# A feed-forward up projection by seven half-size products: nine units instead of four, and their weight sums made by accumulating transfers

## The chip, the cores and the metric

The kernel runs on one core of one Trainium2 chip. The metric is the device time of one execution in microseconds (us), of which the median of three runs is taken. TensorE (PE) multiplies, VectorE (DVE) and ScalarE (ACT) do the elementwise work, GpSimd (POOL) and SyncE (SP) issue transfers: SP on a hardware queue, POOL on a queue whose descriptors software writes.

## The reference

One block of a hybrid model on 528 rows (16 meta tokens and 512 of the sequence), width 1024. All is f32:

```python
xn = rms_norm(h, norm_mix_g[l]); z = xn @ w_in[l]        # a gated linear recurrence and a
...                                                       # retention branch, mixed into h
h = h + mixed @ w_out[l]
xn = rms_norm(h, norm_ffn_g[l])
up = causal_dwconv(xn @ w_up[l], ffn_conv_w[l], ffn_conv_b[l])   # w_up: 1024 x 6144
gate, val = jnp.split(up, 2, axis=-1)
h = h + (jax.nn.gelu(gate) * val) @ w_down[l]             # w_down: 3072 x 1024
out = rms_norm(h, norm_final_g)[:, N_META:]
```

The change is in `xn @ w_up`, in its gate half.

## The kernel before, in words

Every f32 weight is used as two f16 parts, a high part and a remainder, and so is every activation; a product is three matmuls (high x high, high x rest, rest x high). `split` (lines 91 to 94) makes the two parts of a tile: ACT writes the high part (line 92), DVE then the rest (line 93). This is called a cut here.

Weights come in *units* of 1 MB or less, listed in the order of use. `unit_load` (line 187) loads the next unit on SP's queue (`load`, line 104) into a buffer of the pool `wraw` (`raw`, 128 x 2048 f32, two buffers) and queues its cuts, which write tiles of the pool `wsp` (`wt`, ten tiles). The cuts are not made at once: `tick` (line 310), called between the products, makes the next one as long as the tiles from the unit in use onwards are at most `ahead[0]` (6 in the up projection, 8 from j = 10 on). A plain unit takes two tiles and two cuts. The load of a unit is issued when the cuts of the unit before it begin (`u + 2`, line 294).

The up projection runs over j = 0 to 11. Each turn has two units of 8 x 128 rows by 256 columns: one of the gate half (two channels of 128 columns) and one of the value half. A plain turn (lines 1478 to 1490) makes four channels in the same way: `up_conv` runs 48 matmuls of 258 columns on both halves of the rows (line 418) and `conv` the convolution (once ACT, line 1375, twice DVE, line 1377); a gate channel then gets its gelu (line 1391), a value channel is multiplied with its gate (line 1487). `act_forms` (line 1323) cuts the results for the down projection.

In a *fast* turn (j in `FAST_UP`, line 28: 3, 5, 7, 9) the gate unit is computed as a 2 x 2 block product in seven half-size products instead of eight (`up_products`, line 1394): each is 12 matmuls of 258 columns (line 1399). The order on PE is B11, T3, T2, B21, T1, then the first value channel (`ps`), B22, T4, and the second value channel. Names are those of the weight block; B are blocks of the unit, T sums of blocks. Several of them accumulate in one PSUM bank `pa`: after B11 ACT copies it out (`kept`, line 1405), T2 is added on top and copied out (the second `kept`), T1 on top of that (`last`), then B22 (into `g`). DVE adds the pieces (line 1409).

The blocks and sums are made by `fast_steps` (line 237), in place in the raw buffer. top and low are its two halves of rows, left and right its two halves of columns:

```python
return [cut(top, left), cut(low, slice(0, 2 * bc)), sums,
        late(cut(top, slice(0, 2 * bc))), late(cut(low, slice(0, 2 * bc)))]
```

B11 is cut first, then the low half (B21, B22), then `sums` (lines 254 to 258) makes the four sums by three DVE additions (128 x 1024 and twice 128 x 512), and then the top half (T1, T3) and the low half (T4, T2) are cut. Four tiles, 3.5 of them cut. Gate and branch units ahead of the up projection and the units of the down projection are made the same way.

On each engine instructions run in the order in which they stand, and that order is fixed when the program is built. Semaphores make an instruction wait for another engine or for a transfer, and whatever stands behind it on its engine waits too. In the `order` fences below a number behind a name is that of the buffer's allocation, so raw_9953 is one unit's raw buffer and wt_10273 one cut tile.

Of the kernel before, what the change touches and what calls it, by code (L numbers as in the profile page):

```python
# [12 lines left out]
ALU = mybir.AluOpType  # L13
# [10 lines left out]
DFF = 3072  # L24
KF = DFF // P
T0 = NM - 2
TQ = T - T0
FAST_UP = (3, 5, 7, 9)
EPS = 1e-6

SW = 2.0 ** 8
# [20 lines left out]
def hybrid_block_kernel(ctx, tc, x, meta, norm_mix_g, w_in, conv_w, conv_b, rg_a_w, rg_a_b,  # L52
                        rg_x_w, rg_x_b, lam, w_brnn, w_bret, w_out, norm_ffn_g, w_up,
                        fconv_w, fconv_b, w_down, norm_final_g, rope_t, decay_t, out):
    nc = tc.nc
    const = ctx.enter_context(tc.tile_pool(name="const", bufs=1))
    xp = ctx.enter_context(tc.tile_pool(name="xp", bufs=4))
    pieces = ctx.enter_context(tc.tile_pool(name="pieces", bufs=46))
    wraw = ctx.enter_context(tc.tile_pool(name="wraw", bufs=2))
    wsp = ctx.enter_context(tc.tile_pool(name="wsp", bufs=10))  # L60
    work = ctx.enter_context(tc.tile_pool(name="work", bufs=8))
    small = ctx.enter_context(tc.tile_pool(name="small", bufs=4))
# [28 lines left out]
    def split(hi, lo, src, s):  # L91
        a = nc.scalar.activation(hi, src, AF.Copy, scale=s)  # L92
        b = nc.vector.scalar_tensor_tensor(lo, src, s, hi, op0=ALU.mult, op1=ALU.subtract)  # L93
        return a.ins, b.ins
# [3 lines left out]
    def load(dst, src):  # L98

        if last_load[0] is None:  # L100
            last_load[0] = nc.sync.dma_start(dst, src)
        else:
            with tc.issue_after(last_load[0].ins):
                last_load[0] = nc.sync.dma_start(dst, src)


    def kmaj(w, k0, nk, c0, ncol):
        return w[k0 * P:(k0 + nk) * P, c0:c0 + ncol].rearrange("(k p) c -> p k c", p=P)

    units = []  # L110

    def unit(nk, ncol, parts, fast=False):
        units.append((nk, ncol, parts, fast))
        return len(units) - 1

    o_ur, o_ug, o_q, o_k, o_v, o_gr, o_ga, o_gb = 0, 1280, 2560, 3584, 4608, 6656, 8704, 9728
# [1 line left out]
    for i in range(5):  # L118
        u = unit(8, 256, [(0, 0, kmaj(w_in, 0, 8, o_ur + 256 * i, 256))])
# [52 lines left out]
    u_out = [unit(2, 1024, [(0, 0, kmaj(w_out, 2 * a, 2, 0, 1024))]) for a in range(4)]  # L172
    u_up = []
    for j in range(12):
        u_up.append([unit(8, 256, [(0, 0, kmaj(w_up, 0, 8, a * DFF + 256 * j, 256))], fast=a == 0 and j in FAST_UP)
                     for a in range(2)])
    u_dn = []
    for ps_ in range(2):
        for q in range(6):
            rows = w_down[4 * q * P:(4 * q + 4) * P].rearrange("(i j p) c -> p j i c", i=2, j=2)  # L180
# [4 lines left out]
    loaded = []  # L185

    def unit_load(cuts=1):

        nk, ncol, parts, fast = units[len(loaded)]
        raw = wraw.tile([P, 2048], F32, name="raw")  # L190
        n = nk * ncol
        rv = raw[:, :n].rearrange("p (k c) -> p k c", k=nk)
        for k0, c0, ap in parts:
            load(rv[:, k0:k0 + ap.shape[1], c0:c0 + ap.shape[2]], ap)
        loaded.append(len(loaded))
        if fast:
            return fast_steps(rv, nk // 2, ncol // 2)
        hk = nk // 2
        hn = hk * ncol
        tiles = []  # L200

        def step(i, c):
            def run():
                if c == 0:
                    tiles.append(wsp.tile([P, 2, 1024], F16, name="wt"))
                sl = slice(c * hn // cuts, (c + 1) * hn // cuts)
                split(tiles[i][:, 0, sl], tiles[i][:, 1, sl], raw[:, i * hn:(i + 1) * hn][:, sl], SW)
            return run

        wviews.append(lambda a, k, c0, m: tiles[k // hk][:, a, k % hk * ncol + c0:k % hk * ncol + c0 + m])  # L210
        return [step(i, c) for i in range(2) for c in range(cuts)]

    def column_unit():

        _, ncol, parts, _ = units[len(loaded)]
        raw = wraw.tile([P, 2048], F32, name="raw")
        rv = raw.rearrange("p (k c) -> p k c", c=ncol)
        ap = parts[0][2]
        tiles = []

        def fetch(c):
            load(rv[:, :, c * P:c * P + P], ap[:, :, c * P:c * P + P])

        def step(i, c):
            def run():
                if c == 0:
                    tiles.append(wsp.tile([P, 2, 1024], F16, name="wt"))
                tv = [tiles[i][:, a].rearrange("p (k c) -> p k c", c=ncol)[:, :, c * P:c * P + P] for a in range(2)]
                split(tv[0], tv[1], rv[:, 4 * i:4 * i + 4, c * P:c * P + P], SW)
            return run  # L230

        loaded.append(len(loaded))
        wviews.append(lambda a, k, c0, m: tiles[k // 4][:, a, k % 4 * ncol + c0:k % 4 * ncol + c0 + m])
        queue([step(i, c) for c in range(2) for i in range(2)])
        return fetch

    def fast_steps(rv, bk, bc):


        tiles = []  # L240
        top, low = slice(0, bk), slice(bk, 2 * bk)
        left, right = slice(0, bc), slice(bc, 2 * bc)

        def cut(rows, cols):
            def run():
                t = wsp.tile([P, 2, 1024], F16, name="wt")
                src = rv[:, rows, cols]
                n = bk * src.shape[2]
                tv = [t[:, a, :n].rearrange("p (k c) -> p k c", k=bk) for a in range(2)]
                tiles.append(tv)  # L250
                split(tv[0], tv[1], src, SW)
            return run

        def sums():
            pair = rv[:, top].rearrange("p k (h c) -> p h k c", h=2)
            nc.vector.tensor_tensor(pair, pair, rv[:, :, right].rearrange("p (h k) c -> p h k c", h=2), op=ALU.add)  # L256
            nc.vector.tensor_tensor(rv[:, low, right], rv[:, top, left], rv[:, low, right], op=ALU.add)
            nc.vector.tensor_tensor(rv[:, low, left], rv[:, low, left], rv[:, low, right], op=ALU.add)  # L258

        at = {"B11": (0, 0), "B21": (1, 0), "B22": (1, bc), "T1": (2, 0), "T3": (2, bc), "T4": (3, 0), "T2": (3, bc)}  # L260

        def form(nm, a, k):
            i, c0 = at[nm]
            return tiles[i][a][:, k, c0:c0 + bc]

        def late(run):
            def behind():
                with behind_copy():
                    run()
            behind.late = True  # L270
            return behind

        wviews.append(form)
        return [cut(top, left), cut(low, slice(0, 2 * bc)), sums,
                late(cut(top, slice(0, 2 * bc))), late(cut(low, slice(0, 2 * bc)))]

# [4 lines left out]
    def behind_copy():  # L281

        return tc.issue_after(last_keep[0]) if gating[0] and last_keep[0] else nullcontext()

    done = [0]
    ahead = [6]
# [4 lines left out]

    def emit_step():
        u, run = steps[done[0]]
        while len(loaded) < min(u + 2, len(units)):
            queue(unit_load())
        run()
        done[0] += 1

    def queue(new):
        steps.extend((len(loaded) - 1, run) for run in new)  # L300
# [106 lines left out]
    def x_of(hi, lo):  # L407
        tv = (hi, lo)
        return lambda a, k, c0, n: tv[a][:, k, c0:c0 + n]
# [304 lines left out]
    for n in range(NR):  # L714
        ps = acc("ps")
        u, col = u_ug[n // 2], (n % 2) * P
# [587 lines left out]
            x2_whole(-1, None)  # L1304


    ahead[0] = 6
    x2f = x_of(x2h, x2l)
    HU = [(0, 258), (256, 258)]
    acts = []  # L1310
# [140 lines left out]
    def forms(n):  # L1451
        for _ in range(n if forming else 0):
            next(forming[0], None)

    for j in range(12):
        if j == 10:
            ahead[0] = 8
        wg, wu = get(u_up[j][0]), get(u_up[j][1])
        if j == 0:
            forming.append(x2_sums())  # L1460
        gates, vals = [], []
        if j in FAST_UP:
            run = up_products(wg)
            for n in range(5):
                next(run)
                if n in (3, 4):
                    flush(n - 2)
                tick()
            vals.append(up_conv(wu, 0, KF + 2 * j))
            tick()  # L1470
            g1 = gelu(conv(next(run), 2 * j + 1, True), -1.0)
            gates = [gelu(conv(next(run), 2 * j)), g1]
            vals.append(up_conv(wu, P, KF + 2 * j + 1))
            tick()
            for m in range(2):
                nc.vector.tensor_mul(vals[m][:, :SEQ], vals[m][:, :SEQ], gates[m][:, :SEQ])
        else:
            for m in range(2):
                gates.append(gelu(up_conv(wg, m * P, 2 * j + m)))
                (tick_behind_rows if j == 0 else tick)()  # L1480
                forms(1)
            for m in range(2):
                f = 2 * j + m
                if f == KF - 1:
                    psum_layout(bank=6, acc=1)
                cv = up_conv(wu, m * P, KF + f)
                nc.vector.tensor_mul(cv[:, :SEQ], cv[:, :SEQ], gates[m][:, :SEQ])
                vals.append(cv)
                (tick_behind_rows if j == 0 else tick)()
                forms(1)  # L1490
        pending.extend(act_forms(j, vals))
        if j + 1 not in FAST_UP:
            while pending:
                pending.pop(0)()
# [181 lines left out]
```

## Time and profile before

| | |
|---|---|
| Time, median of 3 runs | 1067.66 us (1067.13 to 1067.72) |
| Span of the profiled execution, first to last instruction | 1066.5 us |
| Median beside that span | 1.2 us more |
| DVE, ACT busy over the span | 853.2 us, 587.9 us |
| Mean granted TensorE clock | 0.998 |

The profile gives for each engine its busy time, for each stretch of time the same, the groups of equal instructions by line and shape, who waited for whom, and the chain of waits: the work that ended last, followed back. In a group's row the columns are line, engine, operation, output and input with shapes and count, then busy us and mean ns of one, then the idle time of the engine ahead of it and what ended it. In a row of the stretches the busy times of PE, PE's weight loads, DVE, ACT and POOL follow (with counts), then the granted clock, the share of the 16 DMA engines and GB/s. In a row of the transfers the last two numbers are KB and the median us from issue to landing.

### The profile page before, as it was taken

The page shows a single profiled execution, that of the slowest core. Times are in us where ns is not written, and L with a number is a line of the kernel's source. Part 1 is how long each engine was busy: PE and PEld are TensorE (multiplying, and loading weights), DVE is VectorE, ACT ScalarE, POOL GpSimd, SP SyncE. Part 2 cuts the span into 40 slices and gives each one's busy share as a digit, 9 for nine tenths or more (in the row PEclk, how much of TensorE's full clock was granted, in tenths as well). Part 3 has the DMA queues.
Part 4 walks back from the last instruction along what each step waited for, and adds up shares of the span by engine and source line. Part 5 has one row for each costly group of instructions (what it writes and reads, how often), then busy time and mean ns, then how long its engine had stood idle before and what let it go on. Part 6 is the DMA issues. An engine that isn't in the chain of part 4 may idle for free.

```text
span 1066.5 us, 20995 instructions
## 1 busy us (share of the span) xinstructions
PE 1048.0 (98%) x8995; PEld 851.1 (80%) x8995; DVE 853.2 (80%) x1301; ACT 587.9 (55%) x927; POOL 6.9 (1%) x20
## 2 busy tenths in 40 slices
PE   8999999999999999999999999999999999999997
PEld 6888888865685858887888885588888888888884
DVE  6884799998577878877797776479989897988965
ACT  8568954434364747655554454366566465454442
POOL 2000000000000000000000000000000000000000
PEclk9999999999999999999999999999999999999999
DMA  8341243431022312334433365032432324214322
GB/s 255 104 133 42 80 139 119 160 120 40 2 85 75 120 40 65 119 100 119 129 105 119 115 202 179 1 119 80 159 111 88 119 81 133 67 60 138 101 81 79
DMA packets 108989, 111.49 MB, mean 105 GB/s; under 512 B 5610, under 2 KB 100560, under 8 KB 108896
## 3 DMA queue, kind: packets, MB, share of 16 engines
q1 hardware_dynamic: 108448, 109.74, 32.0%
q8 instruction: 70, 1.15, 0.4%
q10 hardware_dynamic: 160, 0.27, 0.1%
q0 software_dynamic: 288, 0.14, 0.1%
q14 instruction: 23, 0.19, 0.1%
HBM read 108.04 MB, written 2.10 MB: 103 GB/s over the span
## 4 chain that ended last, share of the span: by engine, by line
PE 76%; DVE 13%; ACT 6%; DMA 2%; issue 2%; ACTq 0%; DVEq 0%
PE ps L418 31%; PE P L1512 9%; PE pa L867 7%; PE ps L930 6%; PE ps L1235 4%; DVE wt L93 4%; PE pe L867 3%; PE ps L431 3%; PE pm L418 2%; PE ps L953 2%; PE pa L1399 2%; ACT wt L92 2%; PE pb L867 2%; DVE rnn L665 1%; PE pe L1399 1%
## 5 line engine op out<-in xcount | busy, mean ns | idle before, releaser
L418 PEld LDWEIGHTS <-wt 128*128 128x128 f16 x3840 | 373.2, 97 | 58.2 <-DVE t L759 1.4
L93 DVE SCALAR_TENSOR_TENSOR wt<-raw,wt 128x1024 f16<-128x1024 f32 (+2 forms) x278 | 303.0, 1105 | 58.6 <-ACT wt L92 57.9
L92 ACT ACTIVATE wt<-raw 128x1024 f16<-128x1024 f32 (+2 forms) x278 | 261.4, 962 | 155.7 <-DVE raw L258 30.0
L867 PEld LDWEIGHTS <-wt 128*128 128x128 f16 x2016 | 195.0, 97 | 38.0 <-issue 11.2
L418 PE MATMUL ps<-x2h,wt 128*128 128x258 f16 x1184 | 181.2, 273 | 0.0
L418 PE MATMUL ps<-xh,wt 128*128 128x257 f16 (+2 forms) x1056 | 163.8, 275 | 1.1 <-DVE t L759 1.1
L418 PE MATMUL ps<-x2l,wt 128*128 128x258 f16 x592 | 113.2, 272 | 0.0
L418 PE MATMUL ps<-xl,wt 128*128 128x257 f16 (+2 forms) x528 | 102.2, 275 | 0.0
L1512 PE MATMUL P<-wt,act 128*128 128x256 f16 x792 | 88.3, 273 | 0.0
L1512 PEld LDWEIGHTS <-act 128*128 128x128 f16 x792 | 77.5, 98 | 9.0
L1377 DVE SCALAR_TENSOR_TENSOR cv<-ps,vt,cv 128x512 f32<-128x512 f32 x80 | 59.8, 748 | 22.7 <-ACT cv L1375 21.8
L867 PE MATMUL pa<-xs,wt 128*128 128x257 f16 x576 | 71.6, 273 | 5.1 <-ACT kept L872 4.7
L930 PE MATMUL ps<-wt,xh 128*128 128x512 f16 x256 | 76.1, 379 | 0.4 <-DVE v L93 0.4
L418 PE MATMUL pm<-oa,wt 128*128 128x257 f16 x480 | 55.3, 274 | 0.0
L1375 ACT ACTIVATE cv<-ps,vt,vt 128x512 f32<-128x512 f32 x40 | 30.9, 773 | 34.5 <-PE ps L418 33.8
L930 PE MATMUL ps<-wt,xl 128*128 128x512 f16 x128 | 48.5, 379 | 0.0
L930 PEld LDWEIGHTS <-xh 128*128 128x128 f16 x256 | 24.8, 98 | 29.3 <-issue 0.7
L256 DVE TENSOR_TENSOR raw<-raw 128x1024 f32<-128x1024 f32 x39 | 47.5, 1219 | 0.6
L867 PE MATMUL pa<-ob,wt 128*128 128x257 f16 x384 | 45.7, 274 | 2.0 <-ACT kept L872 1.4
L1235 PE MATMUL ps<-wt,mx 128*128 128x512 f16 x192 | 44.3, 378 | 0.0
L1399 PEld LDWEIGHTS <-wt 128*128 128x128 f16 x336 | 32.6, 97 | 4.4
L1235 PEld LDWEIGHTS <-mx 128*128 128x128 f16 x192 | 17.7, 98 | 18.4
(293 smaller groups left out, 1409.0 us busy)
## 6 DMA issues: line engine op xcount, KB each, us to landing
raw<-in_w_in SPq DMA_DIRECT2D x40, 1024.0 KB, 4.9
raw<-in_w_up SPq DMA_DIRECT2D x24, 1024.0 KB, 5.2
raw<-in_w_down SPq DMA_DIRECT2D x48, 256.0 KB, 3.5
raw<-in_w_branch_ret SPq DMA_DIRECT2D x16, 512.0 KB, 4.7
raw<-in_w_branch_rnn SPq DMA_DIRECT2D x8, 640.0 KB, 4.6
raw<-in_w_out SPq DMA_DIRECT2D x4, 1024.0 KB, 6.2
xin<-in_x SPq DMA_DIRECT2D x4, 512.0 KB, 5.6
raw<-in_w_in SPq DMA_DIRECT2D x4, 512.0 KB, 8.1
```

The source lines that it names most:

```text
L92: a = nc.scalar.activation(hi, src, AF.Copy, scale=s)
L93: b = nc.vector.scalar_tensor_tensor(lo, src, s, hi, op0=ALU.mult, op1=ALU.subtract)
L256: nc.vector.tensor_tensor(pair, pair, rv[:, :, right].rearrange("p (h k) c -> p h k c", h=2), op=ALU.add)
L418: nc.tensor.matmul(ps[:, hf, :n], w(aw, k, col, P), src(ax, k, c0, n), start=k == 0 and (aw, ax) == (0, 0), stop=k == nk - 1 and aw == 1)
L431: mm = nc.tensor.matmul(ps[:, hf, :n], w(aw, k, col, P), src(ax, k, c0, n), start=k == 0 and (aw, ax) == (0, 0), stop=k == KD - 1 and aw == 1)
L867: nc.tensor.matmul(ps[:, :257], ws[k // 4](wf, aw, k % 4), src(xf_, ax, k), start=first and k == 0 and (aw, ax) == (0, 0), stop=k == last_ ...
L930: nc.tensor.matmul(pb, xf(ax, k, XF + j0, nb), w(aw, k % 4, 0, 512), start=i == 0, stop=i == 23)
L1235: nc.tensor.matmul(ps[:, n], mx[k][:, a, c0:c0 + P], wo[k // 2](aw, k % 2, n * 512, 512), start=k == 0 and (a, aw) == (0, 0), stop=k == ks ...
L1375: nc.scalar.activation(vv_, src[:, :, 2:258], AF.Identity, scale=vt2[:, 96 + ch:97 + ch], bias=bias)
L1377: nc.vector.scalar_tensor_tensor(vv_, src[:, :, j:j + 256], vt2[:, 48 * j + ch:48 * j + ch + 1], vv_, op0=ALU.mult, op1=ALU.add)
L1399: nc.tensor.matmul(ps[:, :258], w(wf, aw, k), x2_form(xf_, ax, k), start=first and k == 0 and (aw, ax) == (0, 0), stop=k == 3 and aw == 1, ...
L1512: nc.tensor.matmul(pd[:, 256 * tt:256 * tt + 256], t[:, ax, c0 + tt * P:c0 + tt * P + P], w(wf, aw, i), start=q % 6 == 0 and tt == 0 and i ...
```

## The change

Nine gate units, j = 2 to 10, are made fast instead of four. For the up projection `fast_steps` no longer calls `sums`: each of the four sums is an accumulating transfer on POOL's queue, which adds 128 x 4 x 128 f32 (256 KB) into the raw buffer. One reads its addend from `w_up` in HBM, three from the raw buffer itself. `wraw` gets three buffers instead of two; up projection units are loaded one unit earlier; `ahead` is 10 throughout the up projection; the scratch memory for POOL's descriptors is set to 4096 bytes.

```diff
-FAST_UP = (3, 5, 7, 9)
+FAST_UP = (2, 3, 4, 5, 6, 7, 8, 9, 10)
...
-    wraw = ctx.enter_context(tc.tile_pool(name="wraw", bufs=2))
+    wraw = ctx.enter_context(tc.tile_pool(name="wraw", bufs=3))
...
-        u_up.append([unit(8, 256, [(0, 0, kmaj(w_up, 0, 8, a * DFF + 256 * j, 256))], fast=a == 0 and j in FAST_UP)
+        u_up.append([unit(8, 256, [(0, 0, kmaj(w_up, 0, 8, a * DFF + 256 * j, 256))],
+                            fast=a == 0 and j in FAST_UP, by_dma=True)
...
         if fast:
-            return fast_steps(rv, nk // 2, ncol // 2)
+            return fast_steps(rv, nk // 2, ncol // 2, parts[0][2] if by_dma else None)
...
+        def add_by_dma(rows, cols, src):
+            nc.gpsimd.dma_start(rv[:, rows, cols], src, accum_op=ALU.add)
+
+        def first_sums():
+            cut(top, left)()
+            add_by_dma(top, left, source[:, top, right])
+            add_by_dma(top, right, rv[:, low, right])
+
+        def last_sums():
+            cut(low, slice(0, 2 * bc))()
+            add_by_dma(low, right, rv[:, top, left])
+            add_by_dma(low, left, rv[:, low, right])
...
+        if source is not None:
+            return [first_sums, last_sums, cut(top, slice(0, 2 * bc)), cut(low, slice(0, 2 * bc))]
         return [cut(top, left), cut(low, slice(0, 2 * bc)), sums,
                 late(cut(top, slice(0, 2 * bc))), late(cut(low, slice(0, 2 * bc)))]
...
-        while len(loaded) < min(u + 2, len(units)):
+        while len(loaded) < min(u + (3 if units[u][4] else 2), len(units)):
...
-    ahead[0] = 6
+    ahead[0] = 10
...
-        if j == 10:
-            ahead[0] = 8
...
-    nc = bacc.Bacc("TRN2", target_bir_lowering=False, num_devices=1)
+    nc = bacc.Bacc("TRN2", target_bir_lowering=False, num_devices=1, dynamic_dma_scratch_size=4096)
```

The prediction numbers the four transfers of a unit in the order of this text: 1 adds into (top, left), 2 into (top, right), 3 into (low, right), 4 into (low, left). Lines of the changed kernel lie up to 16 further down.

The order on three engines in the middle of the up projection follows. First ACT, about the two `kept` copies of a fast turn. Before (j = 5; wt_9974 is the first cut of the gate unit two turns on, made from its load):

```order
L1375 ACTIVATE cv_9632<-ps_9583,vt1_93,vt2_94 128x512
L92 ACTIVATE wt_9728<-raw_9669 128x1024
L1405 ACTIVATE kept_9651<-pa_9655 128x258
L92 ACTIVATE wt_9974<-raw_9703 128x512
L1405 ACTIVATE kept_9651<-pa_9655 128x258
L1405 ACTIVATE last_9654<-pa_9655 128x258
```

The change (a turn in the middle; raw_9953 is a gate unit's buffer, raw_10042 the value unit's behind it):

```order
L92 ACTIVATE wt_10250<-raw_9953 128x1024
L1407 ACTIVATE cv_10116<-cv_10116 128x512
L1407 ACTIVATE cv_10134<-cv_10134 128x512
L1391 ACTIVATE cv_10188<-ps_10139,vt1_93,vt2_94 128x512
L1421 ACTIVATE kept_10194<-pa_10198 128x258
L92 ACTIVATE wt_10273<-raw_9953 128x1024
L92 ACTIVATE wt_10304<-raw_10042 128x1024
L1421 ACTIVATE kept_10194<-pa_10198 128x258
L1421 ACTIVATE last_10197<-pa_10198 128x258
```

Between the two `kept` copies stood one small cut of a loaded block; now there stand the cut of the low half's sums (wt_10273, which in the built program waits for transfers 3 and 4 of its unit) and a cut of the value unit. wt_10250 is the cut of the top half's sums, and waits for transfers 1 and 2.

Second, POOL's queue at the units of raw_9953, raw_10212 and raw_10472. Before, POOL's last transfer is one of the small loads at the start of the kernel. The change:

```order
L256 DMA raw_10212<-raw_10212 128x4x128
L256 DMA raw_9953<-raw_9953 128x4x128 x2
L256 DMA raw_10472<-raw_10472 128x4x128
L256 DMA raw_10212<-in_w_up 128x4x128
L256 DMA raw_10212<-raw_10212 128x4x128 x2
```

A transfer 2 stands ahead of the transfers 3 and 4 of the unit before it (the row with x2), and each unit's transfer 1 (from in_w_up) ahead of its own 3 and 4. Third, DVE where a unit's first cut is made. Before, it stands (wt_10482) beside the first of the sums, and T1 to T4 are cut later:

```order
L93 SCALAR_TENSOR_TENSOR wt_10482<-raw_10211,wt_10482 128x512
L256 TENSOR_TENSOR raw_10211<-raw_10211 128x2x4x128
L1409 TENSOR_TENSOR g0_10160<-pb_10216,kept_10159 128x258
L1332 TENSOR_TENSOR d_10230<-cv_10083,cv_10140 128x256
L1333 TENSOR_TENSOR y_10231<-cv_10083 128x256
```

The change, at a first cut (wt_10474) behind the convolution of the first value channel:

```order
L1393 SCALAR_TENSOR_TENSOR cv_10356<-ps_10307,vt2_94,cv_10356 128x512 x2
L93 SCALAR_TENSOR_TENSOR wt_10474<-raw_10212,wt_10474 128x512
L1425 TENSOR_TENSOR g0_10195<-pe_10219,kept_10194 128x258
L1393 SCALAR_TENSOR_TENSOR cv_10376<-g1_10196,vt2_94,cv_10376 128x512
L93 SCALAR_TENSOR_TENSOR wt_10492<-raw_10212,wt_10492 128x1024
```

The sums are gone from DVE, and the first cut stands behind the value convolution of a turn, two turns ahead of the unit's use.

More of the change, by code (lines that the diff above doesn't have):

```diff
@@ L110, in hybrid_block_kernel, with unit @@
     units = []
-    def unit(nk, ncol, parts, fast=False):
-        units.append((nk, ncol, parts, fast))
+    def unit(nk, ncol, parts, fast=False, by_dma=False):
+        units.append((nk, ncol, parts, fast, by_dma))
         return len(units) - 1
@@ L187, in unit_load @@
     def unit_load(cuts=1):
-        nk, ncol, parts, fast = units[len(loaded)]
+        nk, ncol, parts, fast, by_dma = units[len(loaded)]
         raw = wraw.tile([P, 2048], F32, name="raw")
@@ L213, in column_unit @@
     def column_unit():
-        _, ncol, parts, _ = units[len(loaded)]
+        _, ncol, parts, _, _ = units[len(loaded)]
         raw = wraw.tile([P, 2048], F32, name="raw")
@@ L235, in column_unit, with fast_steps @@
         return fetch
-    def fast_steps(rv, bk, bc):
+    def fast_steps(rv, bk, bc, source=None):
         tiles = []
```

## The prediction

> **What bounds the kernel now.** I read the page first (busy shares), then the stretches, then the chain of waits, then the groups by shape, and last the transfers. The page and the stretch that holds the up projection:
>
> ```profile
> PE 1048.0 (98%) x8995; PEld 851.1 (80%) x8995; DVE 853.2 (80%) x1301; ACT 587.9 (55%) x927; POOL 6.9 (1%) x20
> ```
> ```profile
> core 0: us, PE busy (x) PEld busy (x) DVE busy (x) ACT busy (x) POOL busy (x), PEclk, DMA share, GB/s
> 700.00:900.00 200.00, 200.00 (x1803) 174.93 (x1802) 175.97 (x257) 117.36 (x174) 0.00 (x0) 1.00 0.34 111
> ```
>
> PE (TensorE) has no idle time between 700 and 900 us, so this stage is as long as its matmuls; VectorE (DVE) is busy 88% of it and GpSimd (POOL) not at all. The chain of waits of that stretch is PE alone, and shows one turn of the loop over j with seven products (j = 3), then the plain turn j = 4, then the next fast one:
>
> ```profile
> 761.97 1.32 PE pa L1399 x12
> 763.29 1.33 PE pe L1399 x12
> 764.62 1.32 PE pa L1399 x12
> 765.94 1.32 PE pb L1399 x12
> 767.26 1.33 PE pa L1399 x12
> 768.59 5.35 PE ps L418 x48
> 773.93 1.33 PE pa L1399 x12
> 775.26 1.32 PE pe L1399 x12
> 776.58 26.73 PE ps L418 x240
> 803.31 1.32 PE pa L1399 x12
> ```
>
> In order: B11, T3, T2, B21, T1, then the first value channel, then B22, T4, then (in the 26.73) the second value channel, 48 of 240 matmuls or 5.35 us, and the plain turn's 192. A fast turn takes 776.58 + 5.35 - 761.97 = 19.96 us, a plain one 803.31 - 781.93 = 21.38. Fast saves 1.42.
>
> **The matmuls.** j = 2, 4, 6, 8, 10 become fast. Turns 2 to 10 take 4 x 19.96 + 5 x 21.38 = 186.7 us now; nine fast turns would take 179.6. If nothing else moves, that is -7.1 us.
>
> **VectorE and ScalarE.** The groups of 690 to 905 us by shape:
>
> ```profile
> L93 DVE SCALAR_TENSOR_TENSOR wt<-raw,wt 128x1024 f16<-128x1024 f32 x50 | 60.9, 1217 | 3.7 <-ACT wt L92 3.5
> L92 ACT ACTIVATE wt<-raw 128x1024 f16<-128x1024 f32 x49 | 51.4, 1051 | 12.7 <-PE ps L418 7.0 <-DVE raw L256 2.2 <-DMA raw<-in_w_up 2.1
> L1377 DVE SCALAR_TENSOR_TENSOR cv<-ps,vt,cv 128x512 f32<-128x512 f32 x62 | 46.3, 747 | 17.1 <-ACT cv L1375 16.4
> L1375 ACT ACTIVATE cv<-ps,vt,vt 128x512 f32<-128x512 f32 x31 | 23.9, 773 | 26.6 <-PE ps L418 26.0 <-PE ps L431 0.2
> L256 DVE TENSOR_TENSOR raw<-raw 128x1024 f32<-128x1024 f32 x4 | 4.9, 1223 | 0.1
> L1405 ACT ACTIVATE kept<-pa 128x258 f32<-128x258 f32 x8 | 3.0, 380 | 5.3 <-PE pa L1399 5.3
> L258 DVE TENSOR_TENSOR raw<-raw 128x512 f32<-128x512 f32 x4 | 2.8, 689 | 0.1
> L93 DVE SCALAR_TENSOR_TENSOR wt<-raw,wt 128x512 f16<-128x512 f32 x4 | 2.7, 683 | 0.0
> L257 DVE TENSOR_TENSOR raw<-raw 128x512 f32<-128x512 f32 x4 | 2.7, 683 | 0.0
> L1409 DVE TENSOR_TENSOR g<-pb,kept 128x258 f32<-128x258 f32 x4 | 1.7, 421 | 0.1
> ```
>
> Removed from DVE: the sums of four units, 4 x (1.223 + 0.683 + 0.689) = 10.4 us. Added for five more fast units: cuts of 3.5 instead of 2 tiles, (3 x 1.217 + 0.683) - 2 x 1.217 = 1.9 us, and three adds of 0.42, so 5 x 3.16 = 15.8. DVE goes from 176.0 to 181.4 us, in 192.9 instead of 200: 94%. That by itself need not stop PE; the rivals come back to it. ScalarE (ACT) has room (59%).
>
> **The transfers, and what waits for them.** Each fast unit now has four accumulating transfers of 128 x 4 x 128 f32 (256 KB), all on POOL's queue. Number 2 (right top += right low) runs ahead; number 1 needs the cut of the top left quarter finished by DVE; number 3 needs 1 and the low cut; number 4 needs 3. So 1, 3 and 4 follow one another. Let S be the time of the three together, from DVE's end of that first cut to the last landing.
>
> The order on ACT makes S matter. In the built program the ACT cut of the low half's sums waits for transfers 3 and 4, and it stands ahead of the cut of a value unit and of the second "kept" copy; PE's T1 accumulates into the same bank pa and waits for that copy. From there the way back to the next unit's first cut is fixed as well: T1, the first value channel, its convolution on ACT, then on DVE, then DVE's 512 cut, which is what the next unit's transfer 1 waits for. One turn round this loop is one turn of j:
>
> S + 1.05 (ACT cut of sums) + 1.05 (ACT cut of values) + 0.38 (kept) + 1.33 (T1) + 5.35 (value channel) + 0.16 (a matmul's 273 ns less its 110 ns spacing) + 0.77 (ACT conv) + 2 x 0.75 (DVE conv) + 0.68 (DVE cut) = S + 12.3 us.
>
> PE alone needs 19.96. So S up to 7.7 us is free, and above that each microsecond of S is one microsecond of PE idle per turn. Units 4 to 10 run through this loop, which delays T1 of turns 3 to 9: turns 2 to 10 take 2 x 19.96 + 7 x (12.3 + S), and equal today's 186.7 at S = 8.7, or 2.9 us per transfer.
>
> What is one transfer worth? No row shows an accumulating one. The nearest:
>
> ```profile
> raw<-in_w_down SPq DMA_DIRECT2D x48, 256.0 KB, 3.5
> out<-h SPq DMA_DIRECT2D x7, 256.0 KB, 2.3
> v<-in_ffn_conv_w POOLq DMA_DIRECT2D x1, 64.0 KB, 6.2
> v<-in_norm_ffn_g POOLq DMA_DIRECT2D x1, 4.0 KB, 4.9
> ```
> ```profile
> q1 hardware_dynamic: 108448, 109.74, 32.0%
> ```
> ```profile
> L579 POOL DMA_DIRECT2D v<-in_ffn_conv_w x1 | 0.6, 586 | 0.0
> L580 POOL DMA_DIRECT2D v<-in_ffn_conv_w x1 | 0.5, 511 | 0.0
> ```
> ```profile
> L104 SPq DMA_DIRECT2D raw<-in_w_up x24: 367/368/378, 647.5 to 889.5; - x24
> ...
> DMA to landing us min/median/max: 2.6/4.9/9.8
> ```
>
> From below: stores of 256 KB land in 2.3 us and the fastest load in 2.6. From above: POOL's own transfers landed in 4.9 to 6.2, though small; but they ran at the start, with the DMA engines full. My estimate starts from 2.6 and adds three things. POOL's issue: 586 ns for 128 rows against 511 for 16 is 0.67 ns a row, so some 0.85 us for 512 rows against SP's 0.37: +0.5. Packets: 32% of 16 engines over 1066.5 us for 108448 packets is 50 ns for about 1 KB, and here each engine has 32 of 512 B instead of 16 of 1 KB: 0 to 0.8 more, I take 0.4. Reading the destination too: 0 to 1.6, I take 0.8. Together 4.3 us, S = 12.9, a turn of 25.2, and turns 2 to 10 take 216.3: **+29.6 us**. The bounds are -7.1 (2.3 us each) and 2 x 19.96 + 7 x 30.9 - 186.7 = +69.5 (6.2 each). By the Trainium skill ("DMA: Bandwidth & Descriptors", the anatomy of a transfer on the gpsimd path) one costs about 2.0 us plus its bytes over 436 GB/s, 2.6 us here; the sum would then be the full -7.1, and no row of this trace shows POOL so quick.
>
> Unit 3 goes through the same wait at turn 2, but its first cut comes in a plain turn with other work between: 0 to 5.2, I take +2.6. Unit 2's sums fall in turns 0 and 1, where some ten DVE instructions stand between: nothing. POOL has nothing else to do; what its queue holds up is the next unit's transfer 2, needed a turn later. SP's loads of raw buffers now also wait for transfers that read them, a turn ahead of need: nothing, as long as the third buffer is there.
>
> **The clock.** PE would stand idle 5.2 us in each of these turns. At the end of the trace PE stops at 1060 us:
>
> ```profile
> 1060.00:1062.00 2.00, 0.00 (x0) 0.00 (x0) 1.58 (x4) 1.48 (x4) 0.00 (x0) 1.00 0.62 233
> 1062.00:1064.00 2.00, 0.00 (x0) 0.00 (x0) 0.60 (x2) 0.72 (x1) 0.00 (x0) 0.64 0.50 185
> 1064.00:1067.00 3.00, 0.00 (x0) 0.00 (x0) 0.00 (x0) 0.00 (x0) 0.00 (x0) 0.50 0.30 111
> ```
>
> The granted clock is half some 4 us later. How soon it returns no row shows; between nothing and T1 at half rate (1.3 us) a turn, I take the middle: 7 x 0.65 = +4.6. By the Trainium skill ("TensorE: Matmul & The Clock Gate", part 1) an idle window of about 3.4 us halves the clock and as much busy time restores it, which would make this term 7 x 1.7 = 12; the rows agree with its first half.
>
> **Three raw buffers everywhere.** Outside this stage a load can start one unit earlier. The PE waits that this can shorten are
>
> ```profile
> PE pa L867 <- ACT kept L872: 6.2, 8, 1.6
> ...
> PE pa L867 <- ACT last L872: 0.5, 1, 0.5
> ```
>
> so between 0 and -6.7 us (some are ACT behind DVE, not behind a load); I take half, -3.4. The lookahead of 10 tiles moves cuts earlier and adds none.
>
> **Sum**, on the profiled span: 1066.5 + 29.6 + 2.6 + 4.6 - 3.4 = 1099.9. The timed median, 1067.66, lies 1.2 above the span; with it, **1101 us**.
>
> **The rivals.**
> *Quick transfers (the other side).* If an accumulating transfer takes no more than 2.6 us, as loads and stores on the hardware queues do, S is at most 7.7, the loop never closes on PE, and the result is 1067.7 - 7.1 - (0 to 6.7): 1054 to 1061. It decides at 2.6 us; the line between gain and loss is 2.9. For it: the 2.3 and 2.6 above, and in two of the three no trip to HBM. Against it: POOL's 4.9 us for 4 KB. The skill's 2.6 us, above, is this rival. 18%.
> *Transfers at the break-even* (2.6 to 2.9 us each): within a few microseconds of 1067. 5%.
> *Slow ones.* The raw loads of 1 MB share the engines with transfers 1 and 3, and POOL's small loads took up to 6.2 us under load. Above 5.3 us each (S = 15.9, turn 28.2, +50.6, and 7 more with the other terms): 1125 to 1156. 15%.
> *VectorE becomes the bound.* With 94% of its time filled, if it keeps the idle time ahead of its convolutions (17.1 us over 31), 1.1 us a turn, the nine turns lose about 6 of the 7 us: 1063. For: 88% already. Against: that idle time is DVE ahead of PE, and shrinks when it falls behind. 4%.
>
> **How the numbers follow.** The forecast (2.9 to 5.3 us a transfer) has 58%, its own range 1080 to 1125. A measurement of this kernel can tell about 0.2% (2.1 us) from no change. Faster: 18 + 2 from the break-even + 2 of DVE's = 22%; same 3%; slower 75%. The range takes in most of the quick case (down to 1058) and half of the slow one (up to 1140).
>
> **What would show it.** PE between 700 and 930 us at about 80% busy instead of 100%, with "PE pa <- ACT kept" the longest PE wait, some 5 us a turn, seven times; before it "ACT wt <- DMA raw<-raw"; POOL's raw transfers landing in about 4.3 us; T1-to-T1 distances of about 25 us; clock below 1 after the gaps; 60 matmuls fewer. Wrong, if the transfers land in under 2.9 us, if PE stays full there, or if ACT is found waiting for something else than transfers 3 and 4.

## The result, and the profile after

The changed kernel takes 1146.84 us (median of 4 runs, 1144.36 to 1150.96), beside 1067.69 us for the kernel before on the same chip: a ratio of 1.074, 95% interval [1.072, 1.077]. It is slower by 79 us, where 33 were forecast; 1146.84 lies above the range's end of 1140.

The page of after: its busy shares, and its rows of the two kinds of accumulating transfer (count, KB, median us from issue to landing).

```profile
PE 1063.1 (93%) x8935; PEld 854.7 (75%) x8935; DVE 860.1 (75%) x1314; ACT 597.8 (52%) x957; POOL 53.1 (5%) x56
raw<-raw POOLq DMA_DIRECT2D x27, 256.0 KB, 4.2
raw<-in_w_up POOLq DMA_DIRECT2D x9, 256.0 KB, 5.4
```

PE falls from 98% to 93% of a longer span, and no other engine has become the bound. A transfer whose addend is in the raw buffer lands in 4.2 us, the one that reads it from HBM in 5.4 (medians). The stretches of after (PE, weight loads, DVE, ACT and POOL busy, then the granted clock):

```profile
693.00:743.00 50.00, 46.45 (x406) 40.06 (x404) 39.46 (x58) 30.95 (x51) 6.47 (x5) 0.97 0.43 92
820.00:850.00 30.00, 23.89 (x188) 19.52 (x186) 19.40 (x30) 12.54 (x20) 5.13 (x4) 0.84 0.54 108
850.00:880.00 30.00, 21.82 (x181) 18.22 (x180) 18.01 (x27) 12.53 (x20) 5.13 (x4) 0.90 0.53 105
970.00:1000.00 30.00, 29.50 (x266) 25.68 (x265) 27.60 (x41) 19.30 (x30) 0.00 (x0) 1.00 0.35 107
```

Before, PE had no idle time here at a clock of 1.00. Now it is busy 73 to 80% of turns 3 to 9, and fills up again when the last sums are made (970 us). Its waits between 690 and 1000 us (us in total, times, longest), and what ACT waits for:

```profile
PE pa L1415 <- ACT kept L1421: 60.2, 17, 6.4
ACT wt L92 <- DMA raw<-raw: 58.5, 9, 7.6
ACT wt L92 <- DMA raw<-in_w_up: 31.3, 6, 8.3
```

This is the chain that the prediction named: PE waits for a `kept` copy, which stands on ACT behind a cut that waits for a transfer. The chain of waits of one turn of after, from the first value channel of one fast turn to that of the next (start, us, what):

```profile
851.27 5.86 PE ps L434 x48
...
857.15 0.79 ACT cv L1391
...
857.96 0.76 DVE cv L1393
...
858.75 0.76 DVE cv L1393
859.51 0.53 issue
860.03 0.75 POOL raw L256
860.78 6.11 DMA raw<-in_w_up
...
866.96 0.60 issue
867.56 4.20 DMA raw<-raw
871.76 0.39 issue
872.15 4.17 DMA raw<-raw
...
876.41 2.00 ACT wt L92 x2
878.41 0.28 ACT kept L1421
...
878.74 2.74 PE pa L1415 x12
881.47 6.11 PE ps L434 x48
```

Read it as a ring: value channel, its convolution on ACT and DVE, the next unit's first cut (in the 0.53), the issue of a transfer 2 that stands ahead on POOL's queue (the 0.75), transfers 1, 3 and 4 in series, two cuts on ACT, the copy, T1, the next value channel. PE itself stands in it only with T1 and the value channel, 9 us of a turn; the rest of PE's work fits beside it. The timeline of PE in after shows the gaps (in brackets the idle time just before, and what ended it):

```profile
735.34 0.40 PE L434 MATMUL ps<-x2h,wt 128*128 128x258 f16 x2 [3.55 <-DVE cv L1393]
751.11 2.74 PE L1415 MATMUL pa<-x2f,wt 128*128 128x258 f16 x12 [5.97 <-ACT kept L1421]
760.05 2.74 PE L1415 MATMUL pa<-x2f,wt 128*128 128x258 f16 x12 [3.62 <-ACT kept L1421]
```
```profile
870.09 1.49 PE L1415 MATMUL pa<-x2f,wt 128*128 128x258 f16 x12 [2.33 <-ACT kept L1421]
878.74 2.74 PE L1415 MATMUL pa<-x2f,wt 128*128 128x258 f16 x12 [5.84 <-ACT kept L1421]
```
```profile
965.36 2.74 PE L1415 MATMUL pa<-x2f,wt 128*128 128x258 f16 x12 [5.77 <-ACT kept L1421]
```

The T1 of turn 2 starts at 760.05, that of turn 9 at 965.36: (965.36 - 760.05) / 7 = 29.3 us a turn, where 25.2 were forecast. Behind each gap of some 5.8 us T1's 12 matmuls take 2.74 us instead of 1.49: half the rate.

### The profile page after: what moved, and what is told of

The parts are those of the page before. It is cut to its first block, busy times and chain, and to the rows that moved or that the text cites. A ratio compares the mean times of both kernels' runs of the same rounds, so it can differ in the third digit from the quotient of the medians.

```text
span 1144.0 us, 21017 instructions
## 1 busy us (share of the span) xinstructions
PE 1063.1 (93%) x8935; PEld 854.7 (75%) x8935; DVE 860.1 (75%) x1314; ACT 597.8 (52%) x957; POOL 53.1 (5%) x56
## 5 line engine op out<-in xcount | busy, mean ns | idle before, releaser
L93 DVE SCALAR_TENSOR_TENSOR wt<-raw,wt 128x1024 f16<-128x1024 f32 (+2 forms) x288 | 312.6, 1102 | 117.1 <-ACT wt L92 115.9
L92 ACT ACTIVATE wt<-raw 128x1024 f16<-128x1024 f32 (+2 forms) x288 | 269.3, 958 | 211.0 <-DMA raw<-raw 58.5
L434 PE MATMUL ps<-x2h,wt 128*128 128x258 f16 x864 | 139.6, 280 | 6.0 <-DVE cv L1393 6.0
L1415 PE MATMUL pa<-x2f,wt 128*128 128x258 f16 x324 | 51.4, 321 | 60.2 <-ACT kept L1421 60.2
L434 PE MATMUL ps<-x2l,wt 128*128 128x258 f16 x432 | 85.2, 279 | 0.0
L256 POOL DMA_DIRECT2D raw<-raw x27 | 35.3, 1326 | 812.5 <-DVE x2l L93 682.3
L1393 DVE SCALAR_TENSOR_TENSOR cv<-ps,vt,cv 128x512 f32<-128x512 f32 x60 | 44.9, 748 | 20.2 <-ACT cv L1391 19.5
L946 PEld LDWEIGHTS <-xh 128*128 128x128 f16 x256 | 24.8, 98 | 29.3 <-issue 0.7
L270 DVE TENSOR_TENSOR raw<-raw 128x1024 f32<-128x1024 f32 x35 | 42.7, 1220 | 0.6
```

What stands on the lines that cost most here:

```text
L256: nc.gpsimd.dma_start(rv[:, rows, cols], src, accum_op=ALU.add)
L434: nc.tensor.matmul(ps[:, hf, :n], w(aw, k, col, P), src(ax, k, c0, n), start=k == 0 and (aw, ax) == (0, 0), stop=k == nk - 1 and aw == 1)
L946: nc.tensor.matmul(pb, xf(ax, k, XF + j0, nb), w(aw, k % 4, 0, 512), start=i == 0, stop=i == 23)
L1393: nc.vector.scalar_tensor_tensor(vv_, src[:, :, j:j + 256], vt2[:, 48 * j + ch:48 * j + ch + 1], vv_, op0=ALU.mult, op1=ALU.add)
L1415: nc.tensor.matmul(ps[:, :258], w(wf, aw, k), x2_form(xf_, ax, k), start=first and k == 0 and (aw, ax) == (0, 0), stop=k == 3 and aw == 1, ...
```

## The experiments

The theory: the time goes into a ring of waits that the order on ACT closes, with the transfers in series as its longest part. The rivals: nine units as such, the transfers' traffic wherever they stand, VectorE. Each ratio below is to the kernel before, run beside it (medians of 1067.06 to 1067.46 us).

### The sums by VectorE again

```diff
-            return fast_steps(rv, nk // 2, ncol // 2, parts[0][2] if by_dma else None)
+            return fast_steps(rv, nk // 2, ncol // 2)
```

> The changed kernel with the four weight sums of every fast unit made by VectorE again (three additions a unit), no accumulating transfer; nine fast units, three buffers and the lookahead of 10 stay. Loop theory (the 79 us come from waiting for the transfers): PE no longer waits for a kept copy behind a transfer; VectorE then has 19.5 + 2.6 = 22.1 us of work a turn against PE's 19.96, so VectorE sets the pace: about 9 x 22.1 = 199 us for turns 2 to 10 instead of 186.7, in all about 1075 (1062 to 1085). Rival 1, nine fast units cost the time whoever makes their sums (their lookahead, their buffers, the denser order): 1130 or more. Rival 2, VectorE has slack enough even so: about 1057.

1071.06 us, 1.0035 [1.0021, 1.0049] of before. Of the 79 us, 76 go when the transfers go. The edit also brings back the order of steps that belongs to the additions, so it doesn't tell the transfers from the order in which they stand. The stretches (one of six; VectorE is 95 to 98% busy in each) show VectorE as the pace, and PE just short of full, but for 25.95 of 30 us around turn 2:

```profile
830.00:860.00 30.00, 29.37 (x266) 25.56 (x265) 28.75 (x47) 18.86 (x31) 0.00 (x0) 1.00 0.38 122
```

A turn, from the last DVE addition of the first fast turn to that of the last, is (922.6 - 755.7) / 8 = 20.9 us:

```profile
L1425 DVE TENSOR_TENSOR g<-pe,kept x9: 418/418/420, 755.7 to 922.6; 128x258 f32<-128x258 f32 x9
```

The theory had 22.1: VectorE's work with the additions is 20.9 x 28.75 / 30 = 20.0 us a turn, not 19.5 + 2.6.

### Three raw buffers alone

```diff
-    wraw = ctx.enter_context(tc.tile_pool(name="wraw", bufs=2))
+    wraw = ctx.enter_context(tc.tile_pool(name="wraw", bufs=3))
```

> The kernel before with three raw buffers instead of two (and the small descriptor scratch that makes room for the third), nothing else. The trace of after enters the up projection 3.4 us earlier than before does, so the forecast's -3.4 us should be found whole: 1064.3 (1063 to 1066). Rival, the 3.4 us belong to something else that the change moved: no difference, 1067.7.

1064.91 us, 0.9975 [0.9966, 0.9984]. The wait of the earlier stages that the forecast had halved, 6.2 us in 8 waits before, is in this kernel

```profile
PE pa L867 <- ACT kept L872: 2.5, 5, 0.7
```

which is 3.7 us less. Another wait of those stages (PE for DVE's `t`) grew from 1.1 to 2.0 us, and the time fell by 2.4, by the interval 1.7 to 3.6. The term of -3.4 lies within that, near its end.

### Sum 4 by VectorE, the rest by transfers

```diff
-            add_by_dma(low, left, rv[:, low, right])
+            nc.vector.tensor_tensor(rv[:, low, left], rv[:, low, left], rv[:, low, right], op=ALU.add)
```

> The changed kernel with only its fourth transfer (low left += low right) made by VectorE, an addition of 0.69 us that waits for transfer 3; the other three transfers stay. Loop theory: the chain of three transfers in series becomes two and an addition, S falls by about 4.2 + 0.4 - 0.9 = 3.7 us a turn; seven turns and turns 0 to 2 give back about 7 x 3.7 + 5 = 31, and the clock some more: 1105 to 1120. The half clock of the T1 product should partly go. Rival, the cost is in the order on ScalarE alone or in the traffic as such, not in the length of the series: less than 12 us change, 1135 to 1147.

1128.48 us, 1.0574 [1.056, 1.0589]: 18 us less, between the two expectations. The turn, from this row of the groups around `kept`, is (932.6 - 764.3) / 6 = 28.05 us:

```profile
L1425 DVE TENSOR_TENSOR g<-pe,kept x7: 417/418/419, 764.3 to 932.6; 128x258 f32<-128x258 f32 x7
```

The edit was not clean. In the built program the cut of the low sums moved ahead of both `kept` copies, so T2 and B21 entered the ring, and the addition, which waits for transfer 3, stands on DVE ahead of the second value convolution. By the timeline S is 12.2 us in one turn (first cut's end at 795.6, addition's end at 807.8) and 10.4 in the next (823.5 to 833.9), so some 4 less than in after, while the turn fell by 1.3. It speaks for the ring, and can't size it.

### The cuts moved behind the copies

All transfers stay; the cut of the top sums is ordered behind the newest `kept` copy, that of the low sums behind the first value channel's convolution.

```diff
-            return [first_sums, last_sums, cut(top, slice(0, 2 * bc)), cut(low, slice(0, 2 * bc))]
+            return [first_sums, last_sums, behind(cut(top, slice(0, 2 * bc)), last_copy),
+                    held(behind(cut(low, slice(0, 2 * bc)), last_conv))]
```

> The changed kernel with all its transfers, but the two cuts of sums moved on ScalarE: the cut of the top half's sums stands behind the newest kept copy instead of ahead of it, and the cut of the low half's sums behind the convolution of the first value channel, so no kept copy stands behind a transfer. Loop theory (the transfers are as long as before but nothing on PE waits for them): the idle time of PE ahead of T1 and T2 goes; PE is full or VectorE (19.5 us a turn) is just under it: 1055 to 1075, the clock about 1. Rival, the transfers themselves (their traffic, their use of the buffers, the issue on GpSimd) hold the kernel wherever the cuts stand: 1125 to 1150. If a cut now comes too late for its own product instead, the wait should stand at the T1 to T4 products (PE <- DVE wt), between these.

1108.63 us, 1.039 [1.0375, 1.0406]. Both expectations failed: 38 us came back, not 75. The chain of waits tells why, over one turn:

```profile
793.91 5.24 DMA raw<-in_w_up
...
799.82 4.24 DMA raw<-raw
...
804.46 4.19 DMA raw<-raw
...
808.67 1.06 ACT wt L92
...
812.59 0.71 ACT cv L1407
...
813.33 2.08 DVE cv L1410 x3
...
817.14 0.60 DVE wt L93
```

PE no longer stands in the ring, though it still waits for `kept` copies (28.1 us in 8 waits), and the ring is still closed: behind the low cut (808.67) stand a copy, the value cuts and two convolutions on ACT, then convolutions and cuts on DVE, the last of them (817.14) the next unit's first cut, which lets the next transfer 1 start. From 793.3, the end of one first cut, to 817.7, the end of the next, are 24.5 us, 15.4 of them S. Moving the waiting instruction made the ring shorter, but doesn't open it as long as the next unit's first step stands behind it on the same engine.

### The first cuts ahead of the waiting ones

Here each turn orders the first cuts of a unit at its start, then the value cuts, then the cuts of the sums behind the two value convolutions; the next unit's first cut no longer has the whole turn's work between it and the low cut. Once with sum 4 by VectorE (placed behind the cut of the top sums), once with all four transfers.

```diff
-            return [first_sums, last_sums, cut(top, slice(0, 2 * bc)), cut(low, slice(0, 2 * bc))]
+            deferred.extend(behind(cut(rows, slice(0, 2 * bc)), last_conv) for rows in (top, low))
+            return [first_sums, last_sums]
...
+        if not units[len(loaded) - 1][3]:
+            steps.extend((len(loaded) - 1, run) for run in deferred)
+            deferred.clear()
```

> The moved cuts gave back only half, because ScalarE's order still closed a loop without PE: low cut of the sums, then the value cuts and the value convolutions, then the next unit's first cut and its transfer 1. Here that loop is cut too: a unit's first cuts stand at the start of a turn, then the value cuts, then the cut of the top sums behind the first value convolution, the cut of the low sums behind the second; sum 4 is made by VectorE (0.69 us) behind the cut of the top sums. The series of two transfers and an addition, some 11 us, then runs beside a whole turn, and VectorE has 18.4 + 0.7 = 19.1 us a turn, under PE's 19.96. Loop theory: PE full or nearly, 1056 to 1064, below both kernels. Rival (accumulating transfers cost the kernel something wherever the order puts them, by traffic or by buffers): 1080 or more. Rival 2, VectorE at 96% of a turn already binds: about 1068.

> The same order with all four sums as transfers, a series of some 15 us from the first cut. Loop theory: first cut at about 3 us of a turn, last landing at about 19, the low cut at about 20 to 22 and T2, which needs it, at 22.6: just in time or a microsecond or two late each turn, 1055 to 1085, far below the 1108 of the moved cuts. Rival, a transfer costs wherever it stands: 1100 or more.

1079.33 us, 1.0107 [1.0091, 1.0123], and 1082.16 us, 1.013 [1.0114, 1.0145]. With the same four transfers, order alone brings 65 of the 79 us back. The first missed its 1056 to 1064 and came out just under its rival's 1080. Its PE waits from 690 to 1000 us:

```profile
PE pa L1433 <- ACT wt L92: 5.6, 1, 5.6
PE ps L451 <- DVE cv L1411: 4.1, 1, 4.1
PE pa L1433 <- DVE wt L93: 1.9, 7, 0.6
```

The steady turns wait 1.9 us in seven; the two long waits are single, one at turn 2 (766.6) and one behind the last fast turn. With all four transfers PE waits seven times for a `kept` copy, 13.5 us together. The transfers are slower in this order, by the page of that kernel:

```profile
raw<-raw POOLq DMA_DIRECT2D x27, 256.0 KB, 6.5
```

against 4.2 in after. They now run beside other transfers of POOL's queue and the loads; which of the two costs the 2.3 us was not separated, and that these waits come from it is likely, not shown.

### Four units by transfers

```diff
-FAST_UP = (2, 3, 4, 5, 6, 7, 8, 9, 10)
+FAST_UP = (3, 5, 7, 9)
```

> The changed kernel with four fast units (j = 3, 5, 7, 9) as before, their sums by transfers, three buffers and lookahead 10. Loop theory: a plain turn of 21.4 us lies between two fast ones, so a unit's series of 15 us has 41.3 us and does not close on PE turn after turn; PE stays nearly full: 1062 to 1072. Rival, each unit made by transfers costs its 79 / 9 = 8.8 us whatever lies between: 1064 + 35 = about 1100.

1071.18 us, 1.0038 [1.0024, 1.0051], as expected. With a plain turn between two such units PE is full from 770 us on; there is one wait in the whole stage:

```profile
PE ps L434 <- DVE cv L1393: 4.2, 1, 4.2
```

It belongs to the first unit: its low cut waits 7.5 us on ACT (at 748.2), DVE and the value convolutions behind it fall back, and PE finds its bank still taken until 757.9. The value channel behind that wait takes 7.2 us instead of 5.5. Together these are 5.9 of the 6.3 us by which this kernel lies above three buffers alone (1064.91), so no price per unit is left; only the ring and the first unit have one.

### Half the bytes

```diff
-            nc.gpsimd.dma_start(rv[:, rows, cols], src, accum_op=ALU.add)
+            nc.gpsimd.dma_start(rv[:, rows, cols][:, :bk // 2], src[:, :bk // 2], accum_op=ALU.add)
```

> The changed kernel with every accumulating transfer at half its size (128 KB, two of the four row blocks of each sum; the other two are left out). On ScalarE the turns keep their order word for word, so only S changes. In the trace of after a 256 KB transfer lands in 4.2 us; its packets fill the 16 DMA engines for about 2.25 us of that (32.8% of 120 us for 8976 packets, 70 ns each, 32 on an engine), so a half one should land in 3.1, and S fall from about 14.9 to 11: the turn from 29.4 to 25.5, seven turns 27 us, turns 0 to 2 another 4 to 8: 1110 to 1122. Rival, a transfer is nearly all fixed latency (3.9 us or more at half size): 1135 or more. Rival 2, the loop is not S: no change, 1147.

This kernel leaves out half of each sum. 1113.62 us, 1.0432 [1.0414, 1.0449], inside 1110 to 1122. Its page and PE's timeline:

```profile
raw<-raw POOLq DMA_DIRECT2D x27, 128.0 KB, 3.2
```
```profile
777.72 2.74 PE L1415 MATMUL pa<-x2f,wt 128*128 128x258 f16 x12 [3.73 <-ACT kept L1421]
...
828.60 2.74 PE L1415 MATMUL pa<-x2f,wt 128*128 128x258 f16 x12 [3.43 <-ACT kept L1421]
```

These are the T1 of three turns, the middle one left out: (828.60 - 777.72) / 2 = 25.4 us a turn, 25.5 expected. This is the cleanest test of the ring: from turn 3 on ACT's order is that of after, only the transfers are shorter, and the turn follows.

### Without unit 2

```diff
-FAST_UP = (2, 3, 4, 5, 6, 7, 8, 9, 10)
+FAST_UP = (3, 4, 5, 6, 7, 8, 9, 10)
```

> The changed kernel with eight fast units, j = 3 to 10; unit 2 is plain. The forecast gave unit 2's sums, made in turns 0 and 1, no price; the trace of after loses 5.4 us there and 9.6 in turn 2. If a unit made among plain turns has its own price, it only moves to unit 3: one turn of 29.4 becomes 21.4, 1147 - 8 = about 1139 (1136 to 1142). Rival, the start in turns 0 and 1 is dear because unit 2's sums meet the loads and cuts of the stage's beginning: another 5 to 10 us less, 1129 to 1134.

1132.9 us, 1.0619 [1.0605, 1.0634]: 14 us less than after, where one turn of the ring is worth 8. The rival was right: unit 2 costs some 6 us more than another unit. In this kernel PE is full until 740 us (row below), while in after it idled 3.55 us of the stretch 693 to 743:

```profile
690.00:740.00 50.00, 50.00 (x439) 42.69 (x438) 40.88 (x60) 30.80 (x52) 4.39 (x4) 1.00 0.46 120
```

### Three buffers with five or six units, sums by VectorE

The kernel before with three raw buffers and `FAST_UP` = (2, 4, 6, 8, 10), (3, 5, 7, 8, 9, 10) and (3, 5, 7, 9, 10).

> The kernel before with three raw buffers (1064.9 in its own run) and five fast units, j = 2, 4, 6, 8, 10, instead of four, sums by VectorE. A fast turn saves PE 1.42 us; VectorE has some 12% of the stage free: 1063.5 (1062.5 to 1064.5), if the first unit, one turn earlier, finds its weights in time. Rival, VectorE or the load of unit 2 is late at turn 2: 1066 to 1070.

> Three raw buffers, sums by VectorE, fast units j = 3, 5, 7, 8, 9, 10: none before j = 3, since the runs with a unit 2 wait for its copy at turn 2. Two more fast turns than before save PE 2 x 1.42 = 2.8 us on the 1064.9 of three buffers alone: 1062 (1061 to 1063.5). Rival, four fast turns in a row, at some 21 us of VectorE each against PE's 19.96, fall behind more than the lookahead covers, and the start of the down projection pays it: 1065 to 1068.

> The same with j = 3, 5, 7, 9, 10: one more fast turn, 1.42 us: 1063.5 (1062.5 to 1064.5). Rival, as for six units, VectorE late at j = 10 and in the down projection: 1065 to 1067.

With a unit 2: 1068.13 us, 1.0008 [0.9999, 1.0017], the rival; PE waits 2.8 us for a `kept` copy at turn 2, where the kernel with nine units and sums by VectorE waits too (1.6 us). Six units: 1067.13 us, 1.0001 [0.9992, 1.001], the rival too. Its stretches:

```profile
860.00:890.00 30.00, 28.68 (x258) 24.86 (x257) 28.59 (x44) 17.31 (x29) 0.00 (x0) 1.00 0.22 72
920.00:950.00 30.00, 27.50 (x248) 23.82 (x246) 25.40 (x39) 15.82 (x24) 0.00 (x0) 1.00 0.26 86
```

DVE is at 95% in the first of them, where four fast turns follow one another, and PE loses 1.3 and 2.5 us there. Five units without a unit 2: 1064.25 us, 0.9967 [0.9955, 0.998]: 0.3% below the kernel before, and the lowest time of all versions. Its interval overlaps that of three buffers alone, so the fifth unit's 1.4 us isn't shown.

## Why the prediction was wrong in its number, point by point

**The mechanism was right.** The ring that the prediction wrote down is the chain of waits of after, and its rivals fell: quick transfers (4.2 us, not 2.6), VectorE as the bound (75% busy), a change of nothing. The rival of transfers above 5.3 us each didn't happen either, though the time landed in that rival's 1125 to 1156: S is about as long as that rival's 15.9, but made otherwise, so this is no merit of the prediction. Its bounds were also added loosely: with the other terms of the sum unchanged, 2.9 and 5.3 us a transfer give 1071 and 1122, where it wrote 1080 and 1125.

**Where 44 us were missed** (on the profiled span, 1144.0 against 1099.9). In the frame of the forecast four terms of the sum were too small:

*S, forecast 12.9 us* (from the first cut's end to the last landing). This is the largest miss. The estimate of 4.3 us a transfer was right for those within SBUF (4.2). But nothing was put between the three: 0.4 us pass ahead of transfer 1, and 0.6 and 0.4 us between one landing and the next start. And the step "what its queue holds up is the next unit's transfer 2, needed a turn later" had it the wrong way round. In four of the seven turns that transfer 2 is issued first, as the order of the queue ahead of the prediction shows (raw_10472 ahead of raw_10212<-in_w_up), and holds up transfer 1, which the ring needs at once. POOL in one such turn, and in one of the other three:

```profile
860.03 1.27 POOL L256 DMA_DIRECT2D raw<-raw  x1 [16.86 <-DVE cv L1393]
860.78 1.82 POOL L256 DMA_DIRECT2D raw<-in_w_up  x1
...
890.96 1.28 POOL L256 DMA_DIRECT2D raw<-in_w_up  x1 [17.53 <-DVE g L1425]
```

Behind a transfer 2 transfer 1 lands after 5.6 to 6.1 us (four turns); issued first it lands after 4.3 to 4.5 (three turns), so reading HBM alone doesn't make it long. No run moves transfer 2 by itself, and with the moved cuts, where none stands ahead, transfer 1 still takes 4.6 to 5.7 in the turns from 790 us on, so what else slows it stays open. S is 876.3 - 860.1 = 16.2 us in the first of these turns and 14.3 in the second (first cut's end at 890.55, landing at 904.80), 15.2 in the mean of all seven: the miss is 2.3 x 7 = 16 us.

*The clock, forecast 0.65 us a turn.* T1 takes 2.74 us where the sum had 1.33, and the value channel behind it 6.0 in the mean of seven turns (5.54 to 6.62) where it had 5.35 + 0.16: 1.9 us a turn, so 1.25 x 7 = 9 us were missing. The prediction chose the middle between nothing and T1 at half rate; the truth lay above its upper end, since the clock stays low beyond T1. The Trainium skill ("TensorE: Matmul & The Clock Gate", part 1) has idle time of some 3.4 us halve the clock and as much busy time restore it, which the prediction worked out as an estimate of 1.7 a turn. Behind the gaps of 5.8 us the rows agree, with 1.9; but in the kernel without unit 2 twelve matmuls took 2.74 us behind a gap of only 2.18 us, and there the measurement decides.

*Units 2 and 3, forecast 0 and +2.6.* Turn 2 begins at 742.3 in after and 740.6 in before, although the stage began 3.4 us earlier (693.6 against 697.0): turns 0 and 1 lost 5.1. T1 of turn 2 stands 760.05 - 742.3 = 17.8 us into the turn instead of 5.3: +12.5. Together 15 us more than forecast. The step that failed is "some ten DVE instructions stand between: nothing". It looked at DVE; the wait is on ACT, whose cuts of unit 2's sums wait 5.0 and 5.7 us for transfers, with value convolutions behind them:

```profile
721.75 1.06 ACT L92 ACTIVATE wt<-raw 128x1024 f16<-128x1024 f32 x1 [5.01 <-DMA raw<-in_w_up]
731.72 1.06 ACT L92 ACTIVATE wt<-raw 128x1024 f16<-128x1024 f32 x1 [5.71 <-DMA raw<-raw]
```

The run without unit 2 gave 6 us back beyond one turn of the ring. That T2 waits as well as T1 (5.97 us ahead of 751.11) is the second thing missed there.

*Behind the last T1.* From T1 of turn 9 (965.4) to the first product of the down projection's main loop (1027.4) are 62.0 us; before it was 891.1 to 949.9 with a plain turn 10, so 57.4 with a fast one: +4.6, forecast 0. Of these 1.4 are T1 of turn 9 at half rate, 0.5 a wait for a copy in turn 10, and 2.5 a wait of PE for DVE's convolution behind the last fast turn. The kernels with nine and six units and sums by VectorE have that last wait at the same place, with the same 2.5 us, so it is not the transfers'.

16 + 9 + 15 + 4.6 = 44.6 against 44 missed: the sizes hold to about 1 us.

**What held.** -7.1 for the matmuls (60 fewer, as forecast: 8995 to 8935), -3.4 for the three buffers (the stage began 3.4 us earlier), 73 to 80% of PE busy against "about 80%", PE's wait of 5.8 us ahead of T1 against "some 5". By the Trainium skill ("DMA: Bandwidth & Descriptors", the anatomy of a transfer on the gpsimd path), about 2.0 us plus the bytes over 436 GB/s, a transfer of 256 KB would take an estimated 2.6 us. No accumulating transfer here came near that; the measured 4.2 decides.

**What stays open.** Why transfers take 6.5 us in the reordered kernel, whether by the loads or by one another, and how far S could shrink in that order without this. The lookahead of 10 tiles had no run of its own. A version with nine units that is faster than before was not found.

## What to carry to other kernels

When work moves from a busy engine to a transfer, don't ask first how long the transfer takes but what stands behind the instruction that waits for it, on an engine that executes in order. If the next transfer's start stands behind this one's wait, the latency is paid every turn, though, as here, no engine is full; moving the waiting instruction opens the ring only when it moves behind the next turn's first step. And a turn that leaves TensorE idle for 4 us or more, as these did, is to be charged for the matmuls behind the gap at half rate as well, and the first turns of such a loop separately from its steady ones.

## What the runs showed of the hardware

- An accumulating transfer on GpSimd's queue lands in 4.2 us for 256 KB and in 3.2 us for 128 KB, within SBUF: by an estimate from these two sizes 2.2 us fixed and 1.0 us for each 128 KB, so about 130 GB/s. The packets say much the same: between 780 and 900 us of after 8976 packets, nearly all of 512 B, took 32.8% of 16 engines, 120 x 16 x 0.328 / 8976 = 70 ns each, or 117 GB/s with all 16. With the addend in HBM it took 4.6 to 5.4 us at 256 KB (medians of seven kernels), and 4.3 in the quickest steady turn of after.
- Its issue holds POOL for 1.27 us at 256 KB and 1.18 us at 128 KB, so hardly by its bytes; the forecast had 0.85.
- How TensorE's clock falls is not told by the length of a gap alone. The same twelve matmuls in two turns of the kernel with half the bytes, behind gaps of the same length:

```profile
879.59 2.74 PE L1415 MATMUL pa<-x2f,wt 128*128 128x258 f16 x12 [3.19 <-ACT kept L1421]
930.83 1.49 PE L1415 MATMUL pa<-x2f,wt 128*128 128x258 f16 x12 [3.19 <-ACT kept L1421]
```

  Over the kernels here, where twelve such matmuls stood in a row, they took 1.49 us (full rate) behind every gap up to 1.7 us, anything from 1.49 to 2.74 behind gaps of 2.1 to 3.2 us (2.74 behind 2.18, 1.49 behind 3.00), and 2.74 behind every longer one but one (4.54 us, then 2.15).
